# Transposing the attention probabilities of two heads together, and reading both heads' sums after both are written

## The chip, the cores and the metric

The kernel runs on one core of one Trainium2 chip. The metric is device time in microseconds (us) of one execution.

## The reference

Two layers of an encoder block on an input of 256 tokens by 1024, in float32. Cut to what matters:

```python
for l in range(DEPTH):                                   # DEPTH = 2, SEQ = 256, D_MODEL = 1024
    x = x + 0.5 * swiglu(rms_norm(x, ffn1_norm[l]), ...)
    h = rms_norm(x, mix_norm[l])
    z = h @ w_in[l]                                      # q, k, v of both branches, and two gates
    ...
    o_na = neighbourhood_attention(qa, ka, va, na_rpb[l])          # 8 heads of 64
    o_sw = sliding_window_gqa(qs, ks_, vs, t5_bias, sw_sink[l])    # 8 heads of 64, 2 key heads
    g = jax.nn.sigmoid(zg + b_gate[l])
    merged = g[:, :, 0] * (o_na @ w_branch_na[l]) + g[:, :, 1] * (o_sw @ w_branch_sw[l])
    x = x + merged @ w_out[l]
    x = x + 0.5 * swiglu(rms_norm(x, ffn2_norm[l]), ...)
```

Both attentions are, for each head, scores = q k^T + bias, a softmax over 256 keys, and the probabilities times the values.

## The kernel before, in words

Tokens are two tiles (`t`) of 128 rows. Every float32 product is made of three matmuls on rounded halves, high by high, high by low and low by high (`three`, lines 169 to 172); the text calls one such set of three a step. Each weight block (128 partitions by 1024) is loaded into `raw`, rounded by ScalarE (ACT) into `wh`, and VectorE (DVE) subtracts to make `wl` (`split_to`, lines 183 to 185); six blocks of each are in flight.

The order of TensorE's (PE's) instructions is the order in which the program issues them. `tick` counts steps; `defer(lag, key, fn)` issues `fn` when so many steps have passed, and `need` issues it at once where its result is wanted. The other engines' order is set by a scheduler; functions marked `urgent` have high priority there.

In the middle of a layer (`mix`) the projection `z` is computed in units, and the 16 heads' attention is laced between its steps: first eight heads of the sliding window ("sw"), then eight of the neighbourhood ("na"). A head goes through three functions of `attend`:

- `front(h)`: four matmuls make the scores in a PSUM bank `sc`; DVE adds the bias and takes the maximum (line 571), ACT takes exponentials (line 574), DVE inverts the sums and GpSimd (POOL) scales (line 581). The result is the tile `S`, one of `LAG` buffers.
- `turn`, P_LAG = 10 steps later (some heads a little more): four transposes of `S` into a PSUM bank `pt` (line 589), and `split_to` into `ph` by ACT and `pl` by DVE.
- `back`, V_LAG = 7.5 steps later: four matmuls by the values into one half of a PSUM bank `po` (line 603; heads 2j and 2j+1 share the bank). The sum stands in two parts on opposite partitions: ACT copies one part into the tile `o` (line 607) and DVE adds the other (line 608). After the odd head, `split_to` makes `oh`, `ol` of the pair (`oA` for "na", `oB` for "sw").

The pool `ps_acc` has one buffer with tag "po" and one with tag "pt", each a whole PSUM bank. After the last unit come the branch products: `local` multiplies `oB` with `w_bsw`, `grid` multiplies `oA` with `w_bna`, in the order k = 0, 1, 2 for both token tiles and then k = 3, which takes the last pair of "na" heads. Eight units of gates (line 655 on DVE, line 656 on ACT) and the values and keys of "na" (lines 538, 539, 531, 532) are made among the heads too.

Of the kernel before, what the change touches and what calls it, by code (L numbers as in the profile page):

```python
# [11 lines left out]
F32 = mybir.dt.float32  # L12
F32R = mybir.dt.float32r
I32 = mybir.dt.int32
BF16 = mybir.dt.bfloat16
AF = mybir.ActivationFunctionType
ALU = mybir.AluOpType
# [4 lines left out]
P = 128  # L22
# [4 lines left out]
T = S // P  # L27
# [4 lines left out]
DH = 64  # L32
# [7 lines left out]
NEG = -1e30  # L40
RING = 6
RAW = 4
LAG = 3
H_LAG, NORM_LAG, QK_LAG, P_LAG, V_LAG, M_LAG = 7.9, 4.0, 16, 10, 7.5, 5.5
LAST_LAG = 6.1
MORE = {"Q1": 2, ("sw", 4): 1.5, ("na", 4): 2, ("na", 5): 1.5}
# [12 lines left out]
def hybrid_encoder(ctx, tc, x, w_gu1, w_d1, w_in, b_gate, qk_gain, rpb, sink, t5,  # L59
                   w_bna, w_bsw, w_out, w_gu2, w_d2, c_mask, c_band, out):  # L60
    nc = tc.nc
# [6 lines left out]
    ps_acc = ctx.enter_context(tc.tile_pool(name="ps_acc", bufs=1, space=PSUM))  # L68
# [19 lines left out]
    ident = const.tile([P, P], F32, name="ident")  # L88
# [35 lines left out]
    def linked(engine, emit):  # L124
        with ExitStack() as order:
            if engine in chain:
                order.enter_context(tc.issue_after(chain[engine].ins))
            inst = emit()
        if chain:
            chain[engine] = inst  # L130
        return inst
# [23 lines left out]
    def defer(lag, key, fn):  # L155
        later.append((now[0] + lag, len(later), key, fn))
        later.sort(key=lambda e: e[0])

    def need(*keys):
        for e in [e for e in later if e[2] in keys]:  # L160
            later.remove(e)
            e[3]()
# [16 lines left out]
    def flipped(ap):  # L179
        step, n = ap.ap[-1]  # L180
        return bass.AP(tensor=ap.tensor, offset=ap.offset + step * (n - 1), ap=[*ap.ap[:-1], [-step, n]])

    def split_to(hi, lo, src):
        linked("act", lambda: nc.scalar.activation(hi, src, AF.Copy))  # L184
        linked("dve", lambda: nc.vector.tensor_tensor(lo, src, hi.bitcast(F32), ALU.subtract))  # L185
# [301 lines left out]
    def mix(l, n, after):  # L487
        with tc.tile_pool(name="mix", bufs=1) as mp:
# [51 lines left out]

            def attend(name, ins, qT, kh, kl, kidx, bias_of, vcol, ready, oT, sink_l=None):
                oh, ol = oT
                po = [None, None]
                with tc.issue_after(rstd_done[0].ins):
                    bias = [bias_of(0), bias_of(1)]

                def urgent(fn):
                    def run(*args):
                        with tc.high_priority(500):
                            fn(*args)  # L550
                    return run

                @urgent
                def front(h):
                    need(*ins)
                    if h + 2 < NH:
                        bias.append(bias_of(h + 2))
                    b = bias.pop(0)
                    least = FMAX
                    if sink_l is not None:  # L560
                        sk, least = (v[:, sink_l * NH + h:sink_l * NH + h + 1] for v in (snk, nsnk))
                    ps = ps_acc.tile([P, T, S], F32, name="sc", tag="sc", bufs=2)
                    S_ = mp.tile([P, T, S], F32, name="S", tag="S", bufs=LAG)
                    mx = small.tile([P, T], F32, name="mx", tag="mx")
                    sm = small.tile([P, T], F32, name="sm", tag="sm")
                    for t in range(T):
                        for i, k in enumerate((kh, kl)):
                            nc.tensor.matmul(ps[:, t, :], qT[:, h, t * P:(t + 1) * P], k[:, kidx(h), :],  # L568
                                             start=i == 0, stop=i == 1)
                    for t in range(T):  # L570
                        nc.vector.tensor_tensor_reduce(S_[:, t, :], ps[:, t, :], b(t), -1.0, least,  # L571
                                                       ALU.add, ALU.min, mx[:, t:t + 1])
                    for t in range(T):
                        nc.scalar.activation(S_[:, t, :], S_[:, t, :], AF.Exp, bias=mx[:, t:t + 1], scale=-1.0,  # L574
                                             accum_out=sm[:, t:t + 1])
                    if sink_l is not None:
                        es = small.tile([P, T], F32, name="es", tag="es")
                        nc.scalar.activation(es, mx, AF.Exp, bias=sk)
                        nc.vector.tensor_tensor(sm, sm, es, ALU.add)
                    nc.vector.reciprocal(sm, sm)  # L580
                    nc.gpsimd.tensor_tensor(S_, S_, sm.unsqueeze(2).to_broadcast([P, T, S]), ALU.mult)  # L581
                    defer(P_LAG + MORE.get((name, h), 0), (name, h, 0), lambda: turn(h, S_))

                @urgent
                def turn(h, S_):
                    tp = ps_acc.tile([P, T, T, P], F32, name="pt", tag="pt")
                    for t in range(T):
                        for kt in range(T):
                            nc.tensor.transpose(tp[:, kt, t, :], S_[:, t, kt * P:(kt + 1) * P], ident)  # L589
                    ph = mp.tile([P, T, T, P], F32R, name="ph", tag="ph", bufs=2)  # L590
                    pl = mp.tile([P, T, T, P], F32R, name="pl", tag="pl", bufs=2)
                    split_to(ph, pl, tp)
                    defer(V_LAG, (name, h, 1), lambda: back(h, ph, pl))

                @urgent
                def back(h, ph, pl):
                    assert ready()
                    if h % 2 == 0:
                        po[0] = ps_acc.tile([P, 2, T, P], F32, name="po", tag="po")
                        po[1] = mp.tile([P, T, P], F32, name="o", tag="o", bufs=2)  # L600
                    for kt in range(T):
                        for i, p in enumerate((ph, pl)):
                            nc.tensor.matmul(po[0][:, h % 2], vcol(kt, h), p[:, kt], start=kt + i == 0,  # L603
                                             stop=kt + i == 2)
                    a, b = (0, DH) if h % 2 == 0 else (DH, 0)
                    o, ov = po[1], flipped(po[0][:, h % 2])
                    nc.scalar.activation(o[a:a + DH], ov[b:b + DH], AF.Copy)
                    nc.vector.tensor_tensor(o[a:a + DH], o[a:a + DH], ov[a:a + DH], ALU.add)
                    if h % 2:
                        split_to(oh[:, h // 2], ol[:, h // 2], o)  # L610

                for h in range(NH):
                    yield lambda h=h: front(h)
# [49 lines left out]
            def na_bias(h):  # L663
                t2 = mp.tile([P, T2W], F32, name="t2", tag="t2", bufs=2)
                for r in range(2):
# [10 lines left out]
                return lambda t: b[:, t].rearrange("p r c -> p (r c)")  # L676

            sw = attend("sw", ("Q0", "Q1", "K0", "K1"), sqT, *skT, lambda h: h // 4, sw_bias,
                        lambda kt, h: sv[:, kt, h // 4, h % 2 * DH:h % 2 * DH + P], lambda: True, oB, sink_l=l)
            na = attend("na", ("q0", "q1", "k0", "k1"), qT, *kT, lambda h: h, na_bias,  # L680
                        lambda kt, h: va[:, kt, h, :], lambda: "v1" in done, oA)
            step = {
# [8 lines left out]
            heads = iter([*[(sw, h) for h in range(NH)], *[(na, h) for h in range(NH)]])  # L691
            due = 0
            for token in ORDER.split():
                if token[0] == "a":
                    it, h = next(heads)
# [149 lines left out]
```

## Time and profile before

| | us |
|---|---|
| median of 3 runs | 1077.07 |
| lowest, highest | 1076.5, 1078.15 |
| the profiled execution | 1076.94 |
| its span, first to last instruction | 1075.2 |

Engines of the profile: PE is TensorE's matmuls, PEld its weight loads, DVE is VectorE, ACT is ScalarE, POOL is GpSimd, SP is SyncE, whose queue issues the DMAs. A row of the timeline has the start in us from the span's start, the duration, engine, line, operation, output<-inputs, shapes and a count; in brackets the idle time of the engine before it and what ended it. Matmuls are pipelined: a matmul's duration is longer than the distance to the next one, so distances of starts are what counts on PE.

### The profile page before, as it was taken

Reading aid. Unit: us, or ns where it says so; the run is one execution under the profiler, and the core shown is the slowest. Engines: PE = TensorE matmul, PEld = TensorE weight load, DVE = VectorE, ACT = ScalarE, POOL = GpSimd, SP = SyncE. Lnnn points to the kernel's source line nnn. Section 1 sums busy time; section 2 is a strip of 40 time slices with the busy share of each in tenths; the row PEclk is TensorE's granted clock in tenths of the full one; section 3 lists DMA queues with packets and bytes.
Section 4 is the critical chain, followed back from the end, with each engine's and each line's share of the span. In section 5 each row is a group of like instructions: output and inputs, shape, how many; then the busy total and the mean of one; then the engine's idle time right before and its main releaser. Section 6 shows DMA issues by size and latency. Waiting matters only on the chain.

```text
span 1075.2 us, 14749 instructions
## 1 busy us (share of the span) xinstructions
PE 1068.2 (99%) x5125; PEld 890.3 (83%) x5125; DVE 875.8 (81%) x1337; ACT 671.5 (62%) x1014; POOL 116.7 (11%) x118
## 2 busy tenths in 40 slices
PE   8999999999999999999999999999999999999998
PEld 6888888888888888888888888888888888888887
DVE  6678799889886768869977887988898867778696
ACT  6566654788764556565565665557877646566552
POOL 1000120243520000000000000003534000000000
PEclk9999999999999999999999999999999999999999
DMA  7767656765654667756657765657666554776652
GB/s 247 227 214 237 215 190 191 228 194 155 192 188 137 198 199 246 242 168 191 214 162 238 227 213 185 199 153 247 177 195 185 176 175 160 237 231 203 188 196 89
DMA packets 98827, 212.63 MB, mean 198 GB/s; under 512 B 7568, under 2 KB 13744, under 8 KB 98752
## 3 DMA queue, kind: packets, MB, share of 16 engines
q1 hardware_dynamic: 98560, 211.60, 62.3%
q8 instruction: 40, 0.66, 0.2%
q14 instruction: 35, 0.29, 0.1%
q0 software_dynamic: 192, 0.08, 0.1%
HBM read 210.59 MB, written 1.06 MB: 197 GB/s over the span
## 4 chain that ended last, share of the span: by engine, by line
PE 97%; DMA 1%; ACT 1%; DVE 0%; issue 0%; SPq 0%; ACTq 0%
PE g L170 22%; PE g L172 22%; PE g L171 22%; PE acc L170 5%; PE acc L172 5%; PE acc L171 5%; PE tp L320 2%; PE sc L568 1%; PE po L603 1%; PE tp L170 1%; PE tp L171 1%; PE tp L172 1%; PE pt L589 1%; PE tp L201 1%; PE br L170 1%; PE br L171 1%
## 5 line engine op out<-in xcount | busy, mean ns | idle before, releaser
L185 DVE TENSOR_TENSOR wl<-raw,wh 128x1024 fp32r<-128x1024 f32 x336 | 405.7, 1219 | 65.5 <-ACT wh L184 61.8
L184 ACT ACTIVATE wh<-raw 128x1024 fp32r<-128x1024 f32 x336 | 346.7, 1045 | 117.3 <-DMA raw<-in_w_gu 51.4
L170 PE MATMUL g<-wh,xh 128*128 128x512 f32 (+1 forms) x976 | 383.1, 393 | 0.5 <-DVE hh L444 0.5
L172 PE MATMUL g<-wh,xl 128*128 128x512 f32 (+1 forms) x976 | 377.8, 387 | 0.0
L171 PE MATMUL g<-wl,xh 128*128 128x512 f32 (+1 forms) x976 | 377.5, 387 | 0.0
L172 PEld LDWEIGHTS g<-wh,xl 128*128 128x128 f32 x976 | 183.4, 188 | 39.1 <-DVE xl L185 1.5
L170 PEld LDWEIGHTS g<-wh,xh 128*128 128x128 f32 x976 | 183.6, 188 | 33.8 <-DVE hh L444 1.1
L171 PEld LDWEIGHTS g<-wl,xh 128*128 128x128 f32 x976 | 183.7, 188 | 33.4 <-DVE wl L185 0.6
L443 ACT ACTIVATE sg<-g,rs_y 128x256 f32<-128x256 f32 x88 | 41.1, 467 | 89.7 <-PE g L172 77.3
L444 DVE SCALAR_TENSOR_TENSOR hh<-g,rs_y,sg 128x256 f32<-128x256 f32 x88 | 42.3, 481 | 53.0 <-ACT sg L443 53.0
L170 PE MATMUL acc<-wh,hi 128*128 128x512 f32 x180 | 71.2, 395 | 0.0
L171 PE MATMUL acc<-wl,hi 128*128 128x512 f32 x180 | 70.2, 390 | 0.0
L172 PE MATMUL acc<-wh,lo 128*128 128x512 f32 x180 | 70.1, 390 | 0.0
L176 POOL TENSOR_TENSOR rs_y<-ms,mhalf 128x1 f32<-128x1 f32 x12 | 8.1, 678 | 556.5 <-DVE ms L222 548.0
L352 DVE TENSOR_TENSOR u<-raw 128x512 f32<-128x512 f32 x64 | 41.7, 686 | 20.9 <-DMA raw<-in_w_d 20.8
L184 ACT ACTIVATE corner<-raw 128x512 fp32r<-128x512 f32 x32 | 20.1, 629 | 40.4 <-DMA raw<-in_w_d 22.4
L581 POOL TENSOR_TENSOR S<-S,sm 128x512 f32<-128x512 f32 x32 | 37.2, 1161 | 65.6 <-DVE sm L580 38.3
L172 PEld LDWEIGHTS acc<-wh,lo 128*128 128x128 f32 x180 | 33.8, 188 | 7.2
L171 PEld LDWEIGHTS acc<-wl,hi 128*128 128x128 f32 x180 | 33.8, 188 | 6.7
L170 PEld LDWEIGHTS acc<-wh,hi 128*128 128x128 f32 x180 | 33.8, 188 | 6.7
L184 ACT ACTIVATE wh<-v 128x1024 fp32r<-128x1024 f32 x20 | 21.2, 1062 | 28.9 <-DVE v L352 24.5
L574 ACT ACTIVATE S<-S,mx 128x256 f32<-128x256 f32 x64 | 31.9, 499 | 8.0 <-DVE mx L571 7.9
(189 smaller groups left out, 1522.0 us busy)
## 6 DMA issues: line engine op xcount, KB each, us to landing
raw<-in_w_gu SPq DMA_DIRECT2D x176, 512.0 KB, 4.5
raw<-in_w_d SPq DMA_DIRECT2D x100, 512.0 KB, 4.2
raw<-in_w_in SPq DMA_DIRECT2D x64, 512.0 KB, 4.7
raw<-in_w_out SPq DMA_DIRECT2D x16, 512.0 KB, 3.6
bb<-in_b_gate SPq DMA_DIRECT2D x16, 256.0 KB, 3.6
raw<-in_w_bsw SPq DMA_DIRECT2D x8, 512.0 KB, 3.9
raw<-in_w_bna SPq DMA_DIRECT2D x8, 512.0 KB, 3.5
raw<-in_w_d SPq DMA_DIRECT2D x12, 256.0 KB, 2.7
```

The source lines that it names most:

```text
L170: nc.tensor.matmul(ps, xh, wh, start=first, stop=False)
L171: nc.tensor.matmul(ps, xh, wl, start=False, stop=False)
L172: nc.tensor.matmul(ps, xl, wh, start=False, stop=last)
L184: linked("act", lambda: nc.scalar.activation(hi, src, AF.Copy))
L185: linked("dve", lambda: nc.vector.tensor_tensor(lo, src, hi.bitcast(F32), ALU.subtract))
L201: nc.tensor.transpose(tp[:, i, :], xs[t][:, k * P:(k + 1) * P], ident)
L320: nc.tensor.transpose(tp[:, SLOT[t][i], :], hh[:, t, i * P:(i + 1) * P], ident)
L352: sub = lambda to, x, y: nc.vector.tensor_tensor(to, x, y, ALU.subtract)
L443: linked("act", lambda: nc.scalar.activation(sg, ps[:, :FC], AF.Silu, scale=rstd[t]))
L444: linked("dve", lambda: nc.vector.scalar_tensor_tensor(pair[0][:, t], ps[:, FC:], rstd[t], sg, op0=ALU.mult, op1=ALU.mult))
L574: nc.scalar.activation(S_[:, t, :], S_[:, t, :], AF.Exp, bias=mx[:, t:t + 1], scale=-1.0, accum_out=sm[:, t:t + 1])
L581: nc.gpsimd.tensor_tensor(S_, S_, sm.unsqueeze(2).to_broadcast([P, T, S]), ALU.mult)
```

## The change

Three things change, all in `attend`.

- `turn` now takes two heads: it is issued once per pair, P_LAG after the odd head's `front`, makes eight transposes, and puts the even head's into a bank with tag "po" and the odd head's into the bank with tag "pt".
- `back` takes two heads: V_LAG after that, eight matmuls fill both halves of a bank with tag "po"; then come copy and addition of the even head, copy and addition of the odd head, and `split_to`.
- `S` has five buffers in place of three (`LAG`).

```diff
-LAG = 3
+LAG = 5
...
-                    defer(P_LAG + MORE.get((name, h), 0), (name, h, 0), lambda: turn(h, S_))
+                    held.append((h, S_))
+                    if h % 2:
+                        two, held[:] = list(held), []
+                        defer(P_LAG + MORE.get((name, h), 0), (name, h, 0), lambda: turn(two))
...
-                def turn(h, S_):
-                    tp = ps_acc.tile([P, T, T, P], F32, name="pt", tag="pt")
+                def turn(heads):
+                    tps = [ps_acc.tile([P, T, T, P], F32, name="pt", tag=tag) for tag in ("po", "pt")]
+                    for (_, S_), tp in zip(heads, tps):
+                        for t in range(T):
+                            for kt in range(T):
+                                nc.tensor.transpose(tp[:, kt, t, :], S_[:, t, kt * P:(kt + 1) * P], ident)
+                    halves = []
+                    for (h, _), tp in zip(heads, tps):
...
+                        split_to(ph, pl, tp)
+                        halves.append((h, ph, pl))
+                    defer(V_LAG, (name, heads[1][0], 1), lambda: back(halves))
...
+                def back(halves):
+                    po = ps_acc.tile([P, 2, T, P], F32, name="po", tag="po")
+                    o = mp.tile([P, T, P], F32, name="o", tag="o", bufs=2)
+                    for h, ph, pl in halves:
                         for kt in range(T):
...
+                            for i, p in enumerate((ph, pl)):
+                                nc.tensor.matmul(po[:, h % 2], vcol(kt, h), p[:, kt], start=kt + i == 0,
+                                                 stop=kt + i == 2)
+                    for h, _, _ in halves:
+                        a, b = (0, DH) if h % 2 == 0 else (DH, 0)
+                        ov = flipped(po[:, h % 2])
+                        nc.scalar.activation(o[a:a + DH], ov[b:b + DH], AF.Copy)
+                        nc.vector.tensor_tensor(o[a:a + DH], o[a:a + DH], ov[a:a + DH], ALU.add)
+                    split_to(oh[:, h // 2], ol[:, h // 2], o)
```

In the changed kernel the lines of `attend` stand elsewhere: the transposes are line 593, the products line 610, copy and addition lines 615 and 616, the gates' lines 662 and 663.

How it moves instructions, at three places of the first layer. On PE, where heads 2 and 3 of "sw" are multiplied and the next transposes follow (numbers tell tiles apart; `po_2625` holds heads 2 and 3), before:

```order
L603 MATMUL po_2625<-ph_2596,sv_1814 128x256
L603 MATMUL po_2625<-pl_2597,sv_1814 128x256
L603 MATMUL po_2625<-ph_2596,sv_1814 128x256
L603 MATMUL po_2625<-pl_2597,sv_1814 128x256
L170 MATMUL g_2646<-wh_2565,xh1_1793 128x512
L171 MATMUL g_2646<-wl_2566,xh1_1793 128x512
L172 MATMUL g_2646<-wh_2565,xl1_1794 128x512
L170 MATMUL g_2646<-wh_2571,xh1_1793 128x512
L171 MATMUL g_2646<-wl_2572,xh1_1793 128x512
L172 MATMUL g_2646<-wh_2571,xl1_1794 128x512
L589 MATMUL pt_2696<-ident_83,S_2603 128x128 x4
```

The same place now, from the odd head's four products on (the even head's four stand directly ahead):

```order
L610 MATMUL po_2665<-ph_2596,sv_1814 128x256
L610 MATMUL po_2665<-pl_2597,sv_1814 128x256
L610 MATMUL po_2665<-ph_2596,sv_1814 128x256
L610 MATMUL po_2665<-pl_2597,sv_1814 128x256
L170 MATMUL g_2638<-wh_2556,xh1_1793 128x512
L171 MATMUL g_2638<-wl_2557,xh1_1793 128x512
L172 MATMUL g_2638<-wh_2556,xl1_1794 128x512
L170 MATMUL g_2638<-wh_2562,xh1_1793 128x512
L171 MATMUL g_2638<-wl_2563,xh1_1793 128x512
L172 MATMUL g_2638<-wh_2562,xl1_1794 128x512
L593 MATMUL pt_2687<-ident_83,S_2487 128x128 x4
L593 MATMUL pt_2688<-ident_83,S_2603 128x128 x4
```

Two steps lie between products and transposes in both. The transposes were of one head into the bank "pt"; now they are of two heads, and `pt_2687` is a tile with tag "po", the bank in which `po_2665` stood.

On DVE, from the addition of the even head to that of the odd one for heads 0 and 1 of "na", before (`gate` is a gate, `mx` the scores' maximum):

```order
L608 TENSOR_TENSOR o<-o,po 64x256
L655 SCALAR_TENSOR_TENSOR gate_1822<-g,rs_y,bb 128x512
L571 ISA S,mx<-sc,b 128x256
L571 ISA mx 128x1
L571 ISA S,mx<-sc,b 128x256
L571 ISA mx 128x1
L185 TENSOR_TENSOR wl<-raw,wh 128x1024
L580 RECIPROCAL sm<-sm 128x2
L608 TENSOR_TENSOR o<-o,po 64x256
```

and now:

```order
L616 TENSOR_TENSOR o<-o,po 64x256
L571 ISA S,mx<-sc,b 128x256
L571 ISA mx 128x1
L571 ISA S,mx<-sc,b 128x256
L571 ISA mx 128x1
L185 TENSOR_TENSOR wl<-raw,wh 128x1024
L616 TENSOR_TENSOR o<-o,po 64x256
```

The two additions belonged to products that PE made some steps apart; now all eight products are made ahead of the first addition, and the scores' step and a weight's subtraction still stand between the two additions.

On ACT, at the last pair of "na" heads (6 and 7), before:

```order
L607 ACTIVATE o<-po 64x256
L184 ACTIVATE wh<-raw 128x1024
L607 ACTIVATE o<-po 64x256
L184 ACTIVATE oA<-o 128x256
L184 ACTIVATE wh<-raw 128x1024 x3
```

and now (with numbers, since rows read alike):

```order
L615 ACTIVATE o_3369<-po_3368 64x256 x2
L184 ACTIVATE wh_3501<-raw_3499 128x1024
L184 ACTIVATE oA_1820<-o_3369 128x256
L184 ACTIVATE wh_3507<-raw_3505 128x1024
```

A weight block's rounding stands between the last copy and `oA` now; before it stood behind `oA`.

More of the change, by code (lines that the diff above doesn't have):

```diff
@@ L542, in attend @@
                 oh, ol = oT
-                po = [None, None]
+                held = []
                 with tc.issue_after(rstd_done[0].ins):
@@ L581, in front @@
                     nc.gpsimd.tensor_tensor(S_, S_, sm.unsqueeze(2).to_broadcast([P, T, S]), ALU.mult)
-                    defer(P_LAG + MORE.get((name, h), 0), (name, h, 0), lambda: turn(h, S_))
+                    held.append((h, S_))
+                    if h % 2:
+                        two, held[:] = list(held), []
+                        defer(P_LAG + MORE.get((name, h), 0), (name, h, 0), lambda: turn(two))
                 @urgent
-                def turn(h, S_):
-                    tp = ps_acc.tile([P, T, T, P], F32, name="pt", tag="pt")
-                    for t in range(T):
-                        for kt in range(T):
[L589 to L610, printed above, removed]
+                def turn(heads):
[6 more added lines that the diff above has]
+                    for (h, _), tp in zip(heads, tps):
+                        ph = mp.tile([P, T, T, P], F32R, name="ph", tag="ph", bufs=2)
+                        pl = mp.tile([P, T, T, P], F32R, name="pl", tag="pl", bufs=2)
+                        split_to(ph, pl, tp)
+                        halves.append((h, ph, pl))
+                    defer(V_LAG, (name, heads[1][0], 1), lambda: back(halves))
@@ new lines, in back @@
+                @urgent
+                def back(halves):
+                    assert ready()
+                    po = ps_acc.tile([P, 2, T, P], F32, name="po", tag="po")
+                    o = mp.tile([P, T, P], F32, name="o", tag="o", bufs=2)
+                    for h, ph, pl in halves:
+                        for kt in range(T):
+                            for i, p in enumerate((ph, pl)):
[7 more added lines that the diff above has]
+                    split_to(oh[:, h // 2], ol[:, h // 2], o)
```

## The prediction

> **What bounds the kernel now.** I read the page first, then who waits on PE, then the timeline of the attention in the first layer. From the page, the span, PE's busy time and the chain that ended last:
>
> ```profile
> span 1075.2 us, 14749 instructions
> ...
> PE 1068.2 (99%) x5125; PEld 890.3 (83%) x5125; DVE 875.8 (81%) x1337; ACT 671.5 (62%) x1014; POOL 116.7 (11%) x118
> ...
> PE 97%; DMA 1%; ACT 1%; DVE 0%; issue 0%; SPq 0%; ACTq 0%
> ```
>
> The waits of PE, all of them (who waits, for whom, us, times, longest):
>
> ```profile
> PE idle L120 <- DVE blank L115: 1.6, 1, 1.6
> PE tp L201 <- DMA x<-in_x: 1.3, 1, 1.3
> PE g L170 <- DVE hh L444: 0.5, 1, 0.5
> ```
>
> PE is the bound from end to end and has no idle time worth naming; none of these three lies in the attention. So the change can gain only what its PE instructions get cheaper by, and every wait that it puts in front of a PE instruction is added to the time in full.
>
> **The change: what it can gain.** From the timeline of PE, a group of four transposes, one of eight, and one of four score matmuls, each with the matmul after it:
>
> ```profile
> 241.03 0.60 PE L589 MATMUL pt<-ident,S 128*128 128x128 f32 x4
> 241.38 0.49 PE L170 MATMUL g<-wh,xh 128*128 128x512 f32 x1
> 241.71 0.39 PE L171 MATMUL g<-wl,xh 128*128 128x512 f32 x1
> ...
> 242.17 1.03 PE L529 MATMUL tp<-ident,kn 128*128 128x128 f32 x8
> 242.96 0.48 PE L170 MATMUL g<-wh,xh 128*128 128x512 f32 x1
> 243.28 0.39 PE L171 MATMUL g<-wl,xh 128*128 128x512 f32 x1
> ...
> 243.74 0.63 PE L568 MATMUL sc<-skT,sqT 128*128 128x256 f32 x4
> 244.21 0.40 PE L170 MATMUL g<-wh,xh 128*128 128x512 f32 x1
> ```
>
> Four transposes take 0.35 us, and the matmul behind them 0.33 where it otherwise takes 0.23 (next fences), 0.45 in all; eight take 0.79 + 0.09 = 0.88. A merge of two groups saves 0.02, and 16 pairs (8 in each layer) 0.3 us. The products stay as many; the four-matmul group of scores, 0.47 us, shows what a group of that shape costs wherever it stands. One group of transposes starts late today:
>
> ```profile
> 294.40 0.39 PE L172 MATMUL g<-wh,xl 128*128 128x512 f32 x1
> 294.75 0.63 PE L589 MATMUL pt<-ident,S 128*128 128x128 f32 x4
> ```
>
> 0.35 in place of 0.23, 0.12 late; if it goes, and its like in the second layer, that is 0.2 us. The whole gain is at most 0.5 us of 1077.
>
> **What it adds: a wait at the bank "po".** The even head's transposes now go into the bank "po", and there is one. They can start when DVE has read the previous pair's last sum out of it. Today nothing on PE follows such a read closely. This is heads 2 and 3 of "sw" before: last product, ACT's copy, the next transposes (other bank), DVE's addition:
>
> ```profile
> 261.47 0.28 PE L603 MATMUL po<-pl,sv 128*128 128x256 f32 x1
> ...
> 262.82 0.38 ACT L607 ACTIVATE o<-po 64x256 f32<-64x256 f32 x1
> 262.99 0.60 PE L589 MATMUL pt<-ident,S 128*128 128x128 f32 x4
> ...
> 263.48 0.42 DVE L608 TENSOR_TENSOR o<-o,po 64x256 f32<-64x256 f32 x1
> ```
>
> The transposes start 1.52 after the last product, the bank is free only at 263.90, 2.43 after it. Before, that costs nothing, because they write another bank; after the change PE stands there. The read as fast as it goes, and what else the sums need, from the last pair of "na":
>
> ```profile
> 320.65 0.28 PE L603 MATMUL po<-pl,va 128*128 128x256 f32 x1
> 320.77 0.40 PE L170 MATMUL br<-wh,oA 128*128 128x512 f32 x1
> 320.97 0.38 ACT L607 ACTIVATE o<-po 64x256 f32<-64x256 f32 x1 [1.46 <-DVE wl L185]
> ...
> 321.38 0.42 DVE L608 TENSOR_TENSOR o<-o,po 64x256 f32<-64x256 f32 x1 [0.42 <-ACT o L607]
> ...
> 321.83 0.42 ACT L184 ACTIVATE oA<-o 128x256 fp32r<-128x256 f32 x1 [0.49 <-DVE o L608]
> 321.93 0.39 PE L172 MATMUL br<-wh,oA 128*128 128x512 f32 x1
> ...
> 322.28 0.42 DVE L185 TENSOR_TENSOR oA<-o,oA 128x256 fp32r<-128x256 f32 x1 [0.48 <-ACT oA L184]
> ...
> 322.40 1.06 ACT L184 ACTIVATE wh<-raw 128x1024 fp32r<-128x1024 f32 x1 [0.15 <-PE br L172]
> ...
> 322.83 0.39 PE L170 MATMUL br<-wh,oA 128*128 128x512 f32 x1
> ...
> 323.29 0.39 PE L172 MATMUL br<-wh,oA 128*128 128x512 f32 x1
> ```
>
> All times below count from the start of a pair's last product. Copy starts at 0.32, addition 0.41 later, the next ACT step 0.45 after that. In the changed program the even head's copy waits for the last of all eight products, and the odd head's copy waits for the even head's addition, so the four reads go in line: 0.32 + 0.41 + 0.45 + 0.41 + 0.42 = 2.01. If each head's read overlapped the other's products and reads, the last would end as in these rows, at 1.15.
>
> [...]
>
> PE reaches the next transposes after 0.12 and so many steps of 0.69 (two matmuls lie 0.46 apart in the last two rows). The order gives two steps after pairs 2 and 3 of "sw" and pair 3 of "na": 1.50. After pair 1 of "sw" four steps and eight transposes: 3.76. After pair 4 of "sw" four steps and scores: 3.35. After pairs 1 and 2 of "na" three steps and scores: 2.66. After the last pair, the branch's k = 3 is reached at 2.18.
>
> The bare read, 2.01, thus costs 0.5 us at three places; at the last pair 322.25 was when `oA` was ready (1.60), 0.86 more makes 2.46, 0.3 late. That is 1.8 us a layer, 3.6 in all, the least if the reads are in line.
>
> But ACT and DVE work through their queues in order, and other work stands between the two reads. Its durations (heads 0 and 1 of "sw" before, then groups by line; count, total, mean ns):
>
> ```profile
> 249.59 0.28 PE L603 MATMUL po<-pl,sv 128*128 128x256 f32 x1
> ...
> 252.74 1.26 ACT L531 ACTIVATE kh<-tp,qkg 128x512 fp32r<-128x512 f32 x2
> 252.75 0.42 DVE L608 TENSOR_TENSOR o<-o,po 64x256 f32<-64x256 f32 x1
> ...
> 253.68 1.20 DVE L185 TENSOR_TENSOR wl<-raw,wh 128x1024 fp32r<-128x1024 f32 x1
> 254.80 1.40 DVE L532 SCALAR_TENSOR_TENSOR kl<-tp,qkg,kh 128x512 fp32r<-128x512 f32 x2
> ```
>
> ```profile
> L571 DVE CUSTOM_DVE_ANT_0 S<-sc,b 128x256 f32<-128x256 f32 x32 | 12.1, 415 | 0.2
> L655 DVE SCALAR_TENSOR_TENSOR gate<-g,rs_y,bb 128x512 f32<-128x512 f32 x16 | 11.9, 742 | 0.6 <-PE g L172 0.5
> L656 ACT ACTIVATE gate<-gate 128x512 f32<-128x512 f32 x16 | 10.1, 631 | 12.1 <-DVE gate L655 12.1
> ```
>
> Place by place, by the changed order:
> - "sw" pair 2: ACT rounds a weight block between its copies. Its slot comes free with the first step, whose last matmul starts at 0.58, and ACT starts 0.47 behind such a matmul (321.93 to 322.40): 1.05 to 2.11. DVE's `wl` for it stands ahead of the odd addition: to 3.3; addition to 3.7. PE waits 2.2.
> - "sw" pair 3: nothing between: 0.5.
> - "na" pair 3: ACT has a gate (0.63) that waits for DVE's (0.74), which shares DVE with weights. Copy at 1.33 if those are on time, addition to 2.2, wait 0.7; with one late block more. I take 1.0.
> - "sw" pair 1: DVE has `wl` and two `kl` between. The rows of before put the first addition at 3.16 and the end of `kl` at 6.61; a second addition behind it would cost 3.3. With one head's splits less ahead, or ACT and DVE on time, about 1.9. I take 2.4.
> - "sw" pair 4: DVE has the next scores' two steps and a `wl` between. The scores start at 1.50, take 0.63; 0.83 and 1.20 of DVE, addition to 4.5: wait 1.2.
> - "na" pair 1: the same list, but PE is there at 2.66: 1.9.
> - "na" pair 2: a gate on DVE that waits for the second step, 1.74 to 2.48, addition to 2.9: 0.2.
> - Last pair: a weight block is now ahead of `oA` on ACT, 1.75 to 2.81, so `oA` is ready at 3.23, 1.05 late; DVE's `wl` and then the low half end at 4.5, and the third matmul waits 0.8 more: 1.8.
>
> The sum is 11.2 us a layer, 22.4 for two; minus 0.5 gives 21.9.
>
> **Edits costed at nothing.** Two more buffers of `S` and the later turn of even heads: no front waits for `S` now. The products now wait for two heads' `ph`, `pl`: the slowest single head takes from 294.75 above to the end of this row, 5.4 us,
>
> ```profile
> 299.48 0.68 DVE L185 TENSOR_TENSOR pl<-pt,ph 128x512 fp32r<-128x512 f32 x1
> ```
>
> and a second subtraction makes 6.1; eight transposes and eight steps are 6.4. Where that cover fails it is tenths. No DMA is moved past another queue's work.
>
> **Rivals.**
> - *No wait decides; the merge shows.* If the last read ends inside 1.50 us (it ends at 1.15 when the heads' reads don't queue), only the gain is left: 1076.5, not slower. Against it: the program's waits put the reads in line, and 2.01 is over 1.50.
> - *Only the bare reads count*, since ACT and DVE are done with what stands between by then: 3.6 - 0.5, so 1080.0. Against it: the work between depends on steps and scores that PE makes after the products.
> - *ACT and DVE come late everywhere*, as at 262.82 above, where the copy starts at 1.35 in place of 0.32. With 1.03 more at six places and 0.9 at "sw" pair 1, 7.1 a layer: 1113. Against it: PE's waits give both engines time to catch up.
>
> **How the numbers follow.** The profiled execution took 1076.94, its span 1075.2, and the median is 1077.07, 0.13 more. 1076.94 + 21.9 is 1098.8, by the median 1099. I give this 0.75, the bare reads 0.09, late engines 0.10, no wait 0.06. Inside the forecast the sizes are loose: bare reads with only the last pair (3.0 more) and "na" pair 1 (2.8 more) in full give 1086, the low end; the high end, 1112, is just under the late case. Slower by over 0.2% (2.15 us, about what a measurement here can tell from no change) is 0.94, the same 0.04, faster 0.02.
>
> **What would show it.** In the profile after, PE waits for DVE's addition (line 616) at the transposes (line 593), longest after "sw" pairs 1 and 2 and "na" pair 1, and none at the layer's first transposes; PE waits for `oA` at k = 3; PE's busy time itself is unchanged. I am wrong if PE shows no waits on line 616, or if they are all near 0.5, or if the loss sits elsewhere, at the products (line 610) waiting for `pl`.

## The result and the profile after

| | before | after |
|---|---|---|
| median, us | 1077.07 | 1112.5 |
| lowest, highest | 1076.5, 1078.15 | 1110.8, 1113.72 |
| profiled execution, its span | 1076.94, 1075.2 | 1110.8, 1109.0 |

The ratio to the kernel before is 1.0327, with a 95% interval from 1.0309 to 1.0344. The changed kernel is slower, in the way that was forecast, and by more.

The page of the profile after, its span, the engines' busy time, the granted clock in 40 slices of 27.7 us, and the chain that ended last:

```profile
span 1109.0 us, 14733 instructions
...
PE 1076.5 (97%) x5125; PEld 893.6 (81%) x5125; DVE 876.7 (79%) x1337; ACT 671.8 (61%) x1014; POOL 113.9 (10%) x118
...
PEclk9999999999999999999999999999989999999999
...
PE 81%; DVE 9%; ACT 4%; issue 3%; DMA 2%; POOL 0%; DVEq 0%; ACTq 0%; POOLq 0%
```

And what PE waited for:

```profile
PE pt L593 <- DVE o L616: 22.4, 12, 3.1
PE br L170 <- ACT oA L184: 1.6, 2, 0.8
...
PE pt L593 <- POOL S L581: 1.6, 2, 0.8
```

The first row is the forecast wait: transposes that stand until DVE's addition has read the bank "po". It comes 12 times, and the two of the last row are the same wait (there POOL's scaling of the odd head's `S` ended 0.11 us after DVE's addition, and the view names the later; but the even head's transposes come first, their `S` was long ready, and they start 0.15 us after the addition's end, as at the other 12). The chain that ended last went through PE by 97% before; now DVE and ACT are 13% of it. And PE's busy time has risen by 8.3 us though it makes the same 5125 matmuls. More than half of that is something else, and shows in the clock's row as an 8.

Here is the longest wait, after heads 2 and 3 of "sw", from the last product to the transposes (timeline, first layer):

```profile
263.53 0.28 PE L610 MATMUL po<-pl,sv 128*128 128x256 f32 x1
...
264.35 0.38 ACT L615 ACTIVATE o<-po 64x256 f32<-64x256 f32 x1
...
264.63 1.04 ACT L184 ACTIVATE wh<-raw 128x1024 fp32r<-128x1024 f32 x1
264.81 0.39 PE L172 MATMUL g<-wh,xl 128*128 128x512 f32 x1
...
264.89 0.41 DVE L616 TENSOR_TENSOR o<-o,po 64x256 f32<-64x256 f32 x1
...
265.54 1.04 POOL L581 TENSOR_TENSOR S<-S,sm 128x512 f32<-128x512 f32 x1 [4.17 <-DVE sm L580]
265.70 0.38 ACT L615 ACTIVATE o<-po 64x256 f32<-64x256 f32 x1
265.71 1.95 DVE L185 TENSOR_TENSOR wl<-raw,wh 128x1024 fp32r<-128x1024 f32 x1 [0.34 <-ACT wh L184]
267.69 0.42 DVE L616 TENSOR_TENSOR o<-o,po 64x256 f32<-64x256 f32 x1
...
268.26 1.94 PE L593 MATMUL pt<-ident,S 128*128 128x128 f32 x8 [3.06 <-DVE o L616]
```

PE has nothing left at 265.04 and starts again at 268.26. Between the two heads' reads ACT rounds a weight block and DVE subtracts one, as forecast; only then comes the addition that frees the bank. It ends at 268.11, and the transposes start 0.15 us later. The eight transposes behind it take 1.94 us, where eight took 1.03 before. The view of busy time by windows shows why (columns: window, length, busy time and count of PE, PEld, DVE, ACT and POOL, granted clock, DMA share, GB/s):

```profile
264.28:267.69 3.41, 0.92 (x4) 0.40 (x3) 3.04 (x5) 1.75 (x4) 1.04 (x1) 1.00 0.46 122
267.69:271.10 3.41, 2.84 (x13) 2.87 (x14) 1.71 (x4) 1.61 (x3) 0.00 (x0) 0.50 0.62 186
...
800.17:803.58 3.41, 0.65 (x5) 0.45 (x5) 3.35 (x6) 2.23 (x5) 1.97 (x1) 1.00 0.98 345
803.58:806.99 3.41, 3.41 (x14) 3.11 (x13) 2.54 (x7) 1.55 (x3) 0.00 (x0) 0.50 0.25 94
813.82:817.23 3.41, 0.78 (x4) 0.31 (x2) 3.04 (x6) 1.65 (x3) 1.04 (x1) 1.00 0.49 135
817.23:820.64 3.41, 2.96 (x13) 2.96 (x14) 1.71 (x4) 1.61 (x3) 0.00 (x0) 0.50 0.60 173
```

Three times, after a window of 3.41 us in which PE was busy for only 0.65 to 0.92, PE got half its clock (granted clock 0.50) for the next 3.41 us. It was busy for 2.84 + 3.41 + 2.96 = 9.2 us of these at half speed, so 4.6 us went there. Nothing in the prediction has this term.

The sum, measured on PE as the distance between two starts less what it is where nothing waits: 14.9 us a layer at the eight places, the same within 0.1 in both layers, so 29.7; with 4.6 of half clock and less the gain of at most 0.5 it makes 33.8, and the spans differ by 1109.0 - 1075.2 = 33.8.

### The profile page after: what moved, and what is told of

Read it like the earlier page. It is cut to its first block, busy times and chain, and to the rows that moved or that the text cites. A ratio compares the mean times of both kernels' runs of the same rounds, so it can differ in the third digit from the quotient of the medians.

```text
span 1109.0 us, 14733 instructions
## 1 busy us (share of the span) xinstructions
PE 1076.5 (97%) x5125; PEld 893.6 (81%) x5125; DVE 876.7 (79%) x1337; ACT 671.8 (61%) x1014; POOL 113.9 (10%) x118
## 3 DMA queue, kind: packets, MB, share of 16 engines
HBM read 210.59 MB, written 1.06 MB: 191 GB/s over the span
## 4 chain that ended last, share of the span: by engine, by line
PE 81%; DVE 9%; ACT 4%; issue 3%; DMA 2%; POOL 0%; DVEq 0%; ACTq 0%; POOLq 0%
PE g L170 19%; PE g L172 19%; PE g L171 19%; PE acc L172 4%; PE acc L170 4%; PE acc L171 4%; DVE wl L185 4%; ACT wh L184 2%; PE tp L320 2%; PE pt L593 1%; ACT S L574 1%; PE g L237 1%; PE tp L172 1%; PE tp L171 1%; PE tp L170 1%
## 5 line engine op out<-in xcount | busy, mean ns | idle before, releaser
L593 PE MATMUL pt<-ident,S 128*128 128x128 f32 x128 | 19.2, 299 | 24.0 <-DVE o L616 22.4
L172 PEld LDWEIGHTS acc<-wh,lo 128*128 128x128 f32 x180 | 33.8, 188 | 7.2
L171 PEld LDWEIGHTS acc<-wl,hi 128*128 128x128 f32 x180 | 33.8, 188 | 6.7
```

What stands on the lines that cost most here:

```text
L171: nc.tensor.matmul(ps, xh, wl, start=False, stop=False)
L172: nc.tensor.matmul(ps, xl, wh, start=False, stop=last)
```

## The experiments

The theory is that of the prediction with the clock added: PE waits for the bank until DVE's last addition has had its turn, and long stops cost half clock on top. The rival is that taking heads in pairs costs by itself, since ACT and DVE get two heads' work in a lump. All times stand against the kernel before on the same chip (medians 1077.06 to 1077.18).

**Even head's transposes into "pt", odd head's into "po".** PE can make four transposes before it needs the bank.

```diff
-                    tps = [ps_acc.tile([P, T, T, P], F32, name="pt", tag=tag) for tag in ("po", "pt")]
+                    tps = [ps_acc.tile([P, T, T, P], F32, name="pt", tag=tag) for tag in ("pt", "po")]
```

> The changed kernel with the two banks swapped: the even head's transposes go to "pt", the odd head's to "po". The theory of the bank wait: PE makes four transposes (0.44 us) before it needs "po", so each of the 14 waits is 0.44 us shorter, 6.1 us in all; and if the half clock comes from stops of about 3 us, all stops are now under 2.7 us and the 4.7 us of half clock go too: 1112.5 - 10.8 = 1101.7 us. If the half clock has another cause it stays: 1106. The rival, that the pairing itself costs (two heads' splits at once on ACT and DVE): no change, 1112.

Measured: 1109.11, ratio 1.0297 (1.0272 to 1.0322); what PE waited for, first row:

```profile
PE pt L593 <- DVE o L616: 20.2, 10, 2.6
```

The stops got 0.4 to 0.8 us shorter at six places (2.9 to 2.5, 3.2 to 2.8, 1.0 to 0.2, 2.1 to 1.8, 2.1 to 1.7, 0.4 to 0), and one grew: that after pair 3 of "na", from 1.3 to 2.2, where DVE comes to the first addition 0.33 us later and ACT rounds the even head's `ph` between the two copies. The trace has six windows of half clock in place of three, with no wait over 2.6 us by the row above; it is of the slowest of the four executions (1112.75, clock 0.990), and the other three have clocks of 0.994 and 0.995, as the changed kernel has. The theory holds for most waits and not for the sum: shorter stops of this size do not make the half clock go away.

**A bank of its own for the even head** (the idle bank pool of the other transposes).

```diff
-                    tps = [ps_acc.tile([P, T, T, P], F32, name="pt", tag=tag) for tag in ("po", "pt")]
+                    tps = [pool.tile([P, T, T, P], F32, name="pt", tag=tag) for pool, tag in ((ps_tp, "tp"), (ps_acc, "pt"))]
```

> The changed kernel with the even head's transposes in a bank of the two-bank pool of line 69 (tag "tp") in place of "po"; all else as changed, the order on PE too. The theory of the bank wait: the waits at the transposes (26 us) and the half clock (4.7 us) go, the late oA of the last pair (1.7 us a layer) stays: about 1080 to 1081 us. The rival, that the pairing itself costs: most of the loss stays, over 1100.

Measured: 1087.5, ratio 1.0093 (1.0078 to 1.0108), clock 1.000. PE's waits:

```profile
PE pt L593 <- DVE kl L532: 3.0, 2, 1.5
PE pt L593 <- POOL S L581: 2.7, 2, 1.4
```

Waiting for line 616 is gone, and with it 25.0 of the 35.4 us: the wait at "po" and its half clock are shown as the main cause. Four other places remain, these two and two that wait for `oA`. Between starts they make 1.65, 1.53, 0.45 and 1.71 us a layer, 10.7 in all, where the kernel before is 10.3 us faster. The first comes from the experiment itself (the bank taken has readers too). The second is new: head 7's `S` of "sw" comes late.

**Products of two heads together, transposes head by head as before.** Both sums are read after both are written; `ph` and `pl` have three buffers.

```diff
-                    defer(V_LAG, (name, h, 1), lambda: back(h, ph, pl))
+                    held.append((h, ph, pl))
+                    if h % 2:
+                        two, held[:] = list(held), []
+                        defer(V_LAG, (name, h, 1), lambda: back(two))
```

> The kernel before with one part of the change: the products of two heads together and both reads behind them; transposes head by head in "pt" as before, three buffers of ph and pl, three of S. The theory of the bank wait: no transposes stand behind the read, so only the last pair's late oA is left, 1.7 us a layer: about 1080.5 us. The rival, that reading two sums in line costs at every pair: over 1095.

Measured: 1087.6, ratio 1.0094 (1.0079 to 1.0109). PE waits, beside `oA` as in the kernel above, for:

```profile
PE pt L589 <- POOL S L581: 3.9, 2, 2.0
```

Here too I expected less. The transposes are no longer held by the bank, but head 7's `S` is late here as well, by 2.1 us a layer, and the granted clock is 0.998 in all four executions, where it was 0.999 to 1.000 with a bank of its own. On POOL the bias of a later head stands ahead of it:

```profile
272.10 1.17 POOL L678 TENSOR_TENSOR b<-t,mask 128x512 f32<-128x512 f32 x1 [7.76 <-DVE sm L580]
...
273.24 2.23 POOL L581 TENSOR_TENSOR S<-S,sm 128x512 f32<-128x512 f32 x2
```

At this point the rival stood as well as the theory: two kernels without the bank wait were both 10 us slow.

**Five buffers of `S` alone** (the kernel before, with the one number changed).

```diff
-LAG = 3
+LAG = 5
```

> The kernel before with five buffers of rows S in place of three and nothing else. Both theories: 1077, no difference over 0.2%.

Measured: 1077.26, ratio 0.9999 (0.9989 to 1.0008). This part of the change shows no effect on the time.

**Products two steps earlier.**

```diff
-H_LAG, NORM_LAG, QK_LAG, P_LAG, V_LAG, M_LAG = 7.9, 4.0, 16, 10, 7.5, 5.5
+H_LAG, NORM_LAG, QK_LAG, P_LAG, V_LAG, M_LAG = 7.9, 4.0, 16, 10, 5.5, 5.5
```

> The changed kernel with V_LAG 5.5 in place of 7.5: a pair's products are issued two steps (about 1.4 us) earlier, everything else in place. Theory (PE waits for the bank until DVE's last addition has had its turn, so what counts is the distance from the products to the next transposes): each wait at line 593 gets up to 1.4 us shorter, a layer's waits go from 14.9 to about 5 us, the stops over 2 us and the half clock behind them go; 1087, up to 1094 if the products now wait for pl of the odd head. Rival (the wait is made by the reads' own queue and moves with the products): no wait gets shorter, 1112, or more if the products wait for pl.

Measured: 1093.32, ratio 1.0151 (1.0137 to 1.0165), clock 1.000. PE's waits:

```profile
PE pt L593 <- DVE o L616: 9.5, 10, 1.9
...
PE po L610 <- DVE pl L185: 0.9, 2, 0.5
```

The waits for line 616 fell from 22.4 to 9.5 and the half clock went. It is 6 us over the theory's number and inside its range: two waits got shorter by less than two steps (2.9 to 2.1, and 1.3 to 1.2 after pair 3 of "na"), the last pair's 1.71 did not move, and the products wait for `pl` by 0.6 a layer. The upper end was meant for that last wait, which is only 1.2 of the 6 us. The rival that no wait gets shorter is out.

**PE kept at work in the two longest stops.** Sixteen transposes of no use, into the other bank, ahead of those of heads 2, 3 and heads 4, 5 of "sw".

```diff
+                    if name == "sw" and heads[1][0] in (3, 5):
+                        for _ in range(16):
+                            nc.tensor.transpose(tps[1][:, 0, 0, :], heads[0][1][:, 0, :P], ident)
```

> The changed kernel with 16 transposes of no use ahead of the transposes of heads 2, 3 and of heads 4, 5 of "sw" (the two longest stops, 2.9 and 3.2 us), into the other bank, which is free there: 1.74 us of PE work inside a stop that is there anyway, so that PE is idle for 1.2 to 1.5 us in place of 2.9 to 3.2. Theory (the three stretches of half clock come from these stops and cost 1.5 to 1.7 us each beside the waits): the waits' ends stay, the half clock goes, 1112.5 - 4.7 = 1107.8; up to 1109.5 if one stretch moves behind another stop. Rival (the half clock has nothing to do with the stops): 1112.5 with three stretches of half clock. If the added transposes are not hidden: up to 1112.5 + 4 x 1.74 = 1119.5.

Measured: 1107.85, ratio 1.0286 (1.0266 to 1.0305). The stop shown above, now:

```profile
265.06 1.91 PE L592 MATMUL pt<-ident,S 128*128 128x128 f32 x16
268.29 1.06 PE L596 MATMUL pt<-ident,S 128*128 128x128 f32 x8 [1.32 <-DVE o L619]
```

The transposes that count start at 268.29 as they did at 268.26, and eight of them take 1.06 us, not 1.94. PE does 16 transposes more at each of four places, and the median is 4.65 us under that of the changed kernel: the half clock came from these stops. Its four executions go with the granted clock: 1106.2 and 1106.4 us at 0.999, 1109.3 at 0.998, 1111.0 at 0.996. The price fits by the medians; the two profiled spans differ by only 2.5 us, since one window of half clock is left in this profile, behind the stop of 2.1 us after pair 4 of "sw", where the changed kernel had none.

**Sums read head by head, transposes in pairs.** One part of the change undone; PE's order stays.

```diff
-                    for h, _, _ in halves:
                         a, b = (0, DH) if h % 2 == 0 else (DH, 0)
-                        ov = flipped(po[:, h % 2])
-                        nc.scalar.activation(o[a:a + DH], ov[b:b + DH], AF.Copy)
-                        nc.vector.tensor_tensor(o[a:a + DH], o[a:a + DH], ov[a:a + DH], ALU.add)
+                        ov = flipped(po[:, h % 2])
+                        nc.scalar.activation(o[a:a + DH], ov[b:b + DH], AF.Copy)
+                        nc.vector.tensor_tensor(o[a:a + DH], o[a:a + DH], ov[a:a + DH], ALU.add)
```

(The same lines, now inside the loop over the products.)

> The changed kernel with the sum of each head read right behind its own products again (one of the change's parts undone; transposes still two heads together into the banks po and pt). PE's order is the same. Theory (what stretches the wait is other work that ACT and DVE do between the two heads' reads): the scheduler now puts the two reads side by side, so the transposes at line 593 find the bank free at most places, but the odd head's products must wait until the even head's sum is read, 1.15 - 0.12 = about 1.0 us a pair; 8 pairs and the last pair's oA make 9 to 10 us a layer in place of 14.9, and no stop is over 2 us, so no half clock: 1096 to 1099. Rival (the reads themselves are slow, wherever they stand): the waits at line 593 stay near 15 us a layer and 8 us at the products come on top, 1125 or more.

Measured: 1125.74, ratio 1.0454 (1.0439 to 1.0468). PE's first row:

```profile
PE po L610 <- DVE o L615: 32.0, 16, 3.1
```

The theory's number failed by 27 us, and so did its forecast of no half clock: this trace has ten windows of it (granted clock 0.985). The rival's, 1125 or more, is met, but not its picture: as the theory said, the transposes never wait now. But the odd head's products wait at all 16 pairs for the even head's reads, 1.1 to 3.2 us each and not 1.0, since on ACT and DVE the reads have to wait for their turn: after the even head's last product at 248.50 ACT had a rounding and exponentials ahead of the copy, and DVE scores and two weights ahead of the addition.

```profile
248.50 0.28 PE L610 MATMUL po<-pl,sv 128*128 128x256 f32 x1
...
250.64 0.38 ACT L614 ACTIVATE o<-po 64x256 f32<-64x256 f32 x1
...
251.83 0.39 PE L610 MATMUL po<-ph,sv 128*128 128x256 f32 x1 [3.05 <-DVE o L615]
```

So what lies between the two reads is not all of it; what lies ahead of the first counts too. It also shows what writing both sums ahead of reading is good for: with the products of two heads issued together, the kernel is slower without it. The odd head writes other columns of the bank than the even head's reads use; the program's waits stand between them all the same (the 32.0 us above), and no run here shows what happens without them.

**The four places mended.** The kernel with a bank of its own, with the waits left there taken out by moving steps.

```diff
-MORE = {"Q1": 2, ("sw", 4): 1.5, ("na", 4): 2, ("na", 5): 1.5}
+MORE = {"Q1": 2, ("sw", 4): 1.5, ("na", 4): 2, ("na", 5): 1.5, ("sw", 3): 2, ("sw", 7): 2}
...
-                    defer(V_LAG, (name, heads[1][0], 1), lambda: back(halves))
+                    defer(V_LAG - {("na", 5): 1, ("na", 7): 2}.get((name, heads[1][0]), 0), (name, heads[1][0], 1), lambda: back(halves))
```

> The kernel with the even head's transposes in a bank of their own (1087.5), and with what was left there moved: the transposes of heads 2, 3 of "sw" two steps later (they waited 1.65 us for the reads of that bank), those of heads 6, 7 of "sw" two steps later (1.53, S of head 7), the products of the last two pairs of "na" one and two steps earlier (0.45 and 1.71, oA). Theory (the remaining 10.3 us are these four places, 5.3 a layer, and nothing in the pairing costs by itself): 1077 to 1079, the kernel before within 0.2%; the merged transposes can give at most 0.5 us, so not below 1076.5. Rival (taking heads in pairs costs by itself, since ACT and DVE get two heads' work in a lump; moving a wait makes another late): 1083 or more.

Measured: 1080.27, ratio 1.0033 (1.0023 to 1.0043). Three of the four places are gone, and the last pair's is as long as ever:

```profile
321.12 0.42 DVE L616 TENSOR_TENSOR o<-o,po 64x256 f32<-64x256 f32 x1 [0.44 <-ACT o L615]
321.16 0.39 PE L172 MATMUL br<-wh,oA 128*128 128x512 f32 x1
...
321.63 1.06 ACT L184 ACTIVATE wh<-raw 128x1024 fp32r<-128x1024 f32 x1 [0.55 <-PE br L172]
...
322.60 0.40 ACT L184 ACTIVATE oA<-o 128x256 fp32r<-128x256 f32 x1
...
323.05 0.50 PE L170 MATMUL br<-wh,oA 128*128 128x512 f32 x1 [0.82 <-ACT oA L184]
```

Two steps more did not help: the sum is ready at 321.54, but in ACT's queue a weight's rounding stands ahead of `oA`, and that waits for PE (321.16) to free a block.

**The last pair again,** three and a half steps earlier, by which `oA` comes ahead of that rounding.

```diff
-{("na", 5): 1, ("na", 7): 2}
+{("na", 5): 1, ("na", 7): 3.5}
```

> The mended kernel (1080.3) with the products of the last pair of "na" another step and a half earlier (V_LAG less 3.5 in place of 2). There they came two steps earlier and PE still waited 1.71 us a layer for oA, because on ACT a weight's rounding, which waits for PE, still stood between the second copy and oA. With 3.5 the order of ACT has oA ahead of that weight. Theory (the loss is that place in ACT's queue, nothing else is left): 1080.3 - 3.4 = 1076.9, 1076.5 to 1077.5, the kernel before within 0.2%. Rival (the engines take a pair's reads as one lump, so oA is late whatever the order): 1079 to 1080.

Measured: 1076.6 (1076.05 to 1078.03), ratio 0.9995 (0.9987 to 1.0004). PE's waits in full, both in the first 28 us of the kernel and none in the attention:

```profile
PE idle L120 <- DVE blank L115: 1.6, 1, 1.6
PE g L170 <- DVE hh L444: 1.1, 1, 1.1
```

Pairs of heads thus cost nothing by themselves that these runs can tell. The rival falls: what it pointed at were late places in queues, each of which could be moved.

**Transposes in pairs, products head by head** (in the mended kernel, with the products back at their old distance but for the even head's, which come three steps ahead of the odd head's).

```diff
+                    for h, ph, pl in halves:
+                        defer(V_LAG - 3 * (h % 2 == 0), (name, h, 1), lambda h=h, ph=ph, pl=pl: back(h, ph, pl))
```

> Transposes of two heads together in a bank of their own, as in the mended kernel, but products head by head as in the kernel before, the even head's three steps ahead of the odd head's, each read behind its own products. Theory (what the change can gain is in the transposes alone, 0.02 us a pair and the late starts, at most 0.5 us; nothing waits): 1076.5 to 1077.5. Rival (transposing in pairs costs by itself, because the even head waits for the odd one's S and both heads' ph and pl come in a lump): products at line 612 wait for pl, 1079 or more.

Measured: 1089.76, ratio 1.0121 (1.0105 to 1.0136). Expected was no wait; PE's rows say:

```profile
PE po L612 <- DVE o L617: 7.4, 10, 1.7
PE po L612 <- DVE pl L185: 1.8, 2, 0.9
```

It is the wait of the kernel with sums read head by head: three steps (2.1 us) are too little for the reads of the even head, whose sum stands in the same bank as the odd head's. The rival's `pl` is there too, with 1.8 of the 12.7 us. What is asked of the transposes' bank has to be asked of the products' bank as well.

## Why the prediction was wrong in size and right in kind

**What bounds the kernel, and the gain: right.** With every new wait moved away the changed kernel runs at 1076.6, ratio 0.9995; a gain of up to 0.5 us fits, and none is shown.

**The wait at "po": right,** at all seven places, none at a layer's first transposes, and shown by the kernel with a bank of its own.

**The reads in line, 2.01 us from the last product to the end of the last addition: right where ACT is free.** After the last pair of "na" they end 2.01 us behind the product (334.46 to 336.47). After pair 3 of "sw", where nothing stands between:

```profile
277.76 0.28 PE L610 MATMUL po<-pl,sv 128*128 128x256 f32 x1
...
278.41 0.38 ACT L615 ACTIVATE o<-po 64x256 f32<-64x256 f32 x1
...
278.82 0.41 DVE L616 TENSOR_TENSOR o<-o,po 64x256 f32<-64x256 f32 x1 [0.17 <-ACT o L615]
...
279.27 0.38 ACT L615 ACTIVATE o<-po 64x256 f32<-64x256 f32 x1 [0.48 <-DVE o L616]
279.68 0.42 DVE L616 TENSOR_TENSOR o<-o,po 64x256 f32<-64x256 f32 x1 [0.44 <-ACT o L615]
...
280.25 0.96 PE L593 MATMUL pt<-ident,S 128*128 128x128 f32 x7 [0.81 <-POOL S L581]
```

The steps are 0.41, 0.45, 0.41 and 0.42 as forecast. But the copy starts 0.65 after the product, not 0.32, because ACT still had exponentials: 0.33 of the 0.48 by which this place was missed. The other 0.15 is the step from the addition's end (280.10) to the transposes (280.25).

**The place-by-place sum: the step that failed.** Forecast and measured, us a layer:

| after | forecast | measured |
|---|---|---|
| "sw" pair 1 | 2.4 | 2.93 |
| "sw" pair 2 | 2.2 | 3.23 |
| "sw" pair 3 | 0.5 | 0.98 |
| "sw" pair 4 | 1.2 | 2.15 |
| "na" pair 1 | 1.9 | 2.13 |
| "na" pair 2 | 0.2 | 0.40 |
| "na" pair 3 | 1.0 | 1.33 |
| last pair (`oA`) | 1.8 | 1.71 |
| sum | 11.2 | 14.86 |

Seven of eight are too small, by 3.7 us a layer: 7.3 us of the 12.0 between forecast (1098.8) and profiled execution (1110.8). Two terms of the sum were put at nothing without a reason.

The first is the step from DVE to PE. The sum ended each wait with the last addition, but at all 14 waits the transposes start 0.15 us after that addition's end. This is 1.05 us a layer, and most of the miss at "na" pair 2.

The second, 2.6 us a layer, is that wherever I listed the work between the reads I took each engine as free when its work was due. At pair 2 of "sw" the list was right, and ACT's rounding began as forecast, 1.10 after the last product (forecast 1.05). But DVE's subtraction took 1.95 us instead of 1.20, with POOL's scaling under way when it began (the last section has more); the trace of before has such a row too, 1.99 us at 248.92. At pair 4 the list lacked a gate (0.74) ahead of the scores, and DVE was still at two weights when the first sum came:

```profile
286.95 3.10 DVE L185 TENSOR_TENSOR wl<-raw,wh 128x1024 fp32r<-128x1024 f32 x2 [0.29 <-ACT wh L184]
...
287.95 0.28 PE L610 MATMUL po<-pl,sv 128*128 128x256 f32 x1
...
289.98 0.41 DVE L616 TENSOR_TENSOR o<-o,po 64x256 f32<-64x256 f32 x1
290.31 0.74 DVE L662 SCALAR_TENSOR_TENSOR gate<-g,rs_y,bb 128x512 f32<-128x512 f32 x1
```

In the range, the low end is mis-added: "na" pair 1 in full adds 3.8 us (two layers of 1.9), not 2.8, so it should be 1087. Nothing measured turns on it.

**"PE's busy time itself is unchanged": wrong, and the other step that failed.** The half clock, a term that the sum did not have, took 4.6 us more; with the 7.3 that is 11.9 of the 12.0. Of the rise of 8.3 in the page, about 2.7 is no work: at each of 18 stops the last matmul's row runs on for 0.15 us with no next one to overlap it. About 1 us I cannot assign. The trace of before has no stop of this size in the attention, so its price could not be read there; but the prediction never asked what PE's clock does after such a stop.

**The late-engines rival,** priced at 1113, came nearest in number, by luck: the engines were later than forecast by 2.6 us a layer, where it took 7.1, and the step to PE and the clock, which it did not have, made up most of the rest. **The cover of `pl`** held in the changed kernel, as forecast. **The last pair** came out as worked out: a weight's rounding ahead of `oA`.

## What to carry to other kernels

Before two uses share a PSUM bank, count from the last write to the last read of the tenant before, with what is queued on the reading engines both ahead of the first read and between the reads, and the step from the last read to the next write, 0.15 us here; the bare chain of reads, 2.01 us here, is only the floor. Where PE is the bound, a new stop can cost twice, its own time and the clock after it, as three of the four stops of 2.9 to 3.2 us did here (4.6 us of half clock). A loss that looks like the nature of a change may be a few places in a queue: here the last of them fell only when one step's order on ACT changed, and moving it by less had done nothing.

## What the runs showed of the hardware that I had not expected

The half clock came after shorter stops than the about 3 us that I had reckoned with, and by a grid in time. In the trace of the changed kernel its three windows in the attention last 3.41 us each and begin at 267.69, 803.58 and 817.23: the distances, 535.89 and 13.65 us, are 157 and 4 steps of 3.413 us. Of the windows of this grid between 228 and 900 us, half clock followed the three in which PE was busy for 0.65, 0.78 and 0.92 us, and no other; the next in line, with 1.51 us (from 291.57, after pair 4 of "sw"), was followed by full clock. The stop after pair 1 of "sw" lay across two windows in the first layer, with PE busy for 1.96 and 2.10 us in them, and cost no clock; the same stop in the second layer lay almost whole inside one (0.65 us) and did. In the trace of sums read head by head a window with 1.38 us was followed by half clock (from 822.32). Two near cases of one trace, that of the kernel with the clock kept (PE busy for 1.43 and 1.64 us in the window): each window and the one behind it, with half clock and without:

```profile
289.15:292.56 3.41, 1.43 (x11) 0.99 (x10) 3.06 (x9) 2.05 (x7) 2.33 (x2) 1.00 0.92 318
292.56:295.97 3.41, 3.41 (x14) 2.93 (x12) 1.96 (x6) 1.31 (x3) 0.94 (x1) 0.50 0.69 235
...
302.80:306.21 3.41, 1.64 (x10) 1.08 (x8) 2.84 (x9) 3.11 (x7) 2.46 (x2) 1.00 0.43 154
306.21:309.62 3.41, 3.22 (x19) 2.83 (x20) 3.35 (x7) 2.31 (x6) 1.71 (x2) 1.00 0.57 175
```

This was seen and not tried with stops of set length, so what sets the half clock off stays open.

And a subtraction of a weight on DVE (line 185) and POOL's work on whole tiles (scaling of `S`, bias) held each other up, and the one that began first went through. In the attention of the changed kernel they overlap by more than 0.2 us at 14 places. At eight POOL had begun first (as at 265.54 and 265.71 above): the subtraction took 1.56 to 1.98 us in place of 1.22, each longer by the overlap less 0.14. At six the subtraction had begun first: it took its 1.22, and POOL's row 2.04 to 2.10 in place of 1.04 or 1.19. No run here set this order on purpose.
